# Stacks of q and k made for two heads at once and placed by transfers, in a one-core encoder layer

## The chip, the cores and the metric

One core of one Trainium2 chip runs the whole layer in one launch. The metric is the device time of an execution in microseconds; of several runs the median counts. The median of three runs of the kernel before is 787.64 us (787.47 to 788.48).

## What is computed

A post-norm encoder layer on 512 tokens of 1024 channels, in float32. Two token mixers run side by side on one input projection, a learned gate merges them, and a SwiGLU channel mixer follows.

```python
qa, ka, va, qb, kb, vb = jnp.split(h @ w_in[l], SPLITS, axis=-1)
qa = rope_partial(qa, pos); ka = rope_partial(ka, pos)      # 16 query heads, 4 kv heads of 64
qb = rope_partial(qb, pos); kb = rope_partial(kb, pos)      # 3 groups of 4 heads of 64
o_a = windowed_gqa_sink(qa, ka, va, a_sink[l])              # |i-j| <= 128, with a sink logit
o_b = dilated_mixture(qb, kb, vb)                           # (window, dilation) 128/1, 512/4, 2048/16
g_a, g_b = jnp.split(jax.nn.sigmoid(h @ w_gate[l] + b_gate[l]), 2, axis=-1)
y = (g_a * (o_a @ w_br_a[l]) + g_b * (o_b @ w_br_b[l])) @ w_out[l]
h = layer_norm(DN_ALPHA * h + y, ln1_g[l], ln1_b[l])
f = (jax.nn.silu(h @ w_ff_gate[l]) * (h @ w_ff_up[l])) @ w_ff_down[l]
h = layer_norm(DN_ALPHA * h + f, ln2_g[l], ln2_b[l])
```

## The kernel before

Every float32 product is made of reduced-precision parts. An operand x is split into hi (x rounded to the matmul's type, a copy on ScalarE or VectorE) and lo (x - hi, a subtraction on VectorE), and a product is three matmuls: hi x hi, hi x lo, lo x hi (`feat_k`, lines 441 to 456). A unit of weights is 128 output channels of one matrix: two half units of 128x512, each loaded by SP into a staging slot (6 of class "ws") and split into two weight slots (12 of class "whl"). A half unit feeds four steps of three matmuls.

The program's order is not written by hand. `Program.run` (lines 166 to 259) takes all operations with their costs and lists them as they would become ready: each engine takes, of the operations that are ready and whose buffers fit, the one with the smallest priority number. Priority numbers follow the dense products; evacuations stand 100 ahead (`EV`), weight loads and splits 130 ahead (`LOOK`). A transfer by SP is taken to hold the queue for 0.06 us and to be done after the terms of lines 232 to 236:

```python
if e == SP:
    end = now + 0.06
    dma[0] = max(dma[0], now) + 0.45
    dma[1] = max(dma[1], dma[0] + 0.65) + cost
    o.done = dma[1] + 0.9
```

The engines then run their lists in order, and semaphores keep the dependences. `ORDER` (line 75) names the order of the work: q units and k units of mixer A (q1 to q7, k1) and of mixer B (Q and K, pair and group), values (VA, V0, V12), gates (G, g) and the attention units A0 to A3 and B0 to B3.

Slots: 85 slots of 128x512 floats. 10 hold the mixers' results (`oaT`, eight, and `obT`), 16 belong to the attention, 6 and 12 to the weights, and the other 41 are general ("gen"). `fits` (line 147) lets an operation that is not the next in line take a general slot only when `spare` (14) stay free. When the last attention unit is done `free_all` raises the limit to 63 (line 916).

The change touches these parts.

- `q_post` (line 489): `rotate` makes the rotary form R of a unit's two heads, four VectorE operations (lines 471 to 477). A head's stack t holds hi in one half of the partitions and lo in the other. For each head one copy (line 498, shown under the copy helper's lines 321 and 323) and one subtraction (line 501), each on 64 partitions, put them there.
- `k_post` (line 508): for each head two copies of hi into the two halves of t, one subtraction (line 519) and one copy of lo into the other half of kl.
- `scores` (line 528) multiplies a q stack with t and with kl, at lines 535 and 536.
- `split_of` (line 923; copy 925, subtraction 926) splits a result for the merging products. Line 940 does so for mixer A's eight results `oaT`. Their products (lines 944 to 948) are shown at lines 451 to 453 with the operands `sl,sl`.
- A gate that has to wait is stored to HBM (line 853, from SP) and loaded again (line 935).

Of the kernel before, what the change touches and what calls it, by code (L numbers as in the profile page):

```python
# [10 lines left out]
F32R = mybir.dt.float32r  # L11
BF16 = mybir.dt.bfloat16
AF = mybir.ActivationFunctionType
ALU = mybir.AluOpType

P = 128
S = 512
# [4 lines left out]
NR = 4  # L22
# [23 lines left out]
PE, ACT, DVE, POOL, SP = "PE", "ACT", "DVE", "POOL", "SP"  # L46
# [7 lines left out]

N_HALF = 3
N_LAST1, N_LAST = 5, 4
BANKS = dict(dense=3, s=2, tb=2, o=1, d=8)
UNITS = 2
SPIN = 4
# [5 lines left out]
N_WS, N_WHL, N_ATT = 6, 12, 16  # L65
# [3 lines left out]
N_CHUNK, N_PAIR, N_WF, N_WS2, N_WHL1, N_WHL2 = 3, 3, 9, 10, 54, 20  # L69
# [23 lines left out]


class Op:
    __slots__ = ("alts", "fn", "prio", "left", "ready", "succ", "bufs", "new", "done", "eng", "strict", "moves", "hold")


class Program:
# [12 lines left out]
    def buf_of(tok):  # L112
        return tok[0] if isinstance(tok, tuple) else tok

    def op(self, alts, fn, reads=(), writes=(), prio=0.0, after=(), abs_prio=None, moves=0.0):
        o = Op()
        o.alts, o.fn = alts, fn
        o.prio = (self.T + prio if abs_prio is None else abs_prio, len(self.ops))
        o.ready, o.done, o.eng = 0.0, None, None
        deps = set(a for a in after if a is not None)  # L120
        for t in reads:
            deps.update(self.writer.get(t, ()))
        for t in writes:
            deps.update(self.writer.get(t, ()))
            deps.update(self.readers.get(t, ()))
        deps.discard(o)
        for t in reads:
            self.readers.setdefault(t, []).append(o)
        for t in writes:
            self.writer[t] = [o]  # L130
            self.readers[t] = []
        o.bufs, o.new = [], []
        o.strict, o.moves = self.strict, moves
        o.hold = self.hold and prio <= -150
        for t in list(reads) + list(writes):
            b = self.buf_of(t)
            if b not in o.bufs:
                o.bufs.append(b)
                b.users += 1
        o.succ = []  # L140
        o.left = len(deps)
        for d in deps:
            d.succ.append(o)
        self.ops.append(o)
        return o

    def fits(self, o):
        need = {}
        for b in o.bufs:
            if b.tile is None:  # L150
                for key in b.keys:
                    if key in self.limits:
                        need[key] = need.get(key, 0) + 1
        if "gen" in need and self.limits["gen"] - self.used["gen"] - need["gen"] < self.spare:
            while self.line and self.line[0].done is not None:
                self.line.popleft()
            if self.line and self.line[0] is not o:
                return False
        if "whl" in need and o.strict:
            while self.weights and self.weights[0].done is not None:  # L160
                self.weights.popleft()
            if self.weights and self.weights[0] is not o:
                return False
        return all(self.used[k] + n <= self.limits[k] for k, n in need.items())
# [106 lines left out]
def dve(n, fast=False, extra=0.0):  # L271
    return 0.069 + (0.00052 if fast else 0.00104) * n + extra
# [7 lines left out]
def hybrid_layer(ctx: ExitStack, tc: tile.TileContext, wpack, xT, xtok, sink, bgate,  # L280
                 ln1g, ln1b, ln2g, ln2b, ropec, ropes, maska, maskb, identd, out):
    nc = tc.nc
# [5 lines left out]
    N_SLOT = 85  # L288
    pr = Program({"slot": N_SLOT, "bank": 8, **BANKS,
                  "ws": N_WS, "whl": N_WHL, "att": N_ATT, "gen": N_SLOT - 10 - N_ATT - N_WS - N_WHL,  # L290
                  "unit": UNITS, "st": 4, "x4": 4, "wf": N_WF})
    op = pr.op
# [7 lines left out]
    def slot(dt=F32, cls=None):  # L300
        cls = cls or "gen"
        return Buf("slot", cls, lambda: slab.tile([P, S], dt, tag="slab", bufs=N_SLOT, name=name("sl")))
# [16 lines left out]
    def copy(eng, dst, src):  # L319
        if eng == ACT:  # L320
            nc.scalar.activation(dst, src, AF.Copy)  # L321
        else:
            nc.vector.tensor_copy(dst, src)

    def f32(ap):
        return ap.bitcast(F32)
# [11 lines left out]
    def cp_alts(n, ps=False, cut=0.0):  # L338
        return [(ACT, act(n, ps) + cut), (DVE, dve(n, not ps) + cut)]

    CUT = 0.12
# [73 lines left out]
    for j in range(KD):  # L415
        st, ap = slot(F32, "xs"), FIRST["x"][j]

        for c0, c1 in ((0, S // 2), (S // 2, S)) if j == 0 else ((0, S),):
            w, sk = c1 - c0, (st, c0)
            th, tl = [(b, j, c0) if j == 0 else (b, j) for b in (xh4[j // 4], xl4[j // 4])]  # L420
            eng, dma = (ACT, nc.scalar) if j == 0 and c0 == 0 else (SP, nc.sync)
# [3 lines left out]
               reads=[sk], writes=[th], abs_prio=ap)  # L425
            op([(DVE, dve(w))], lambda e, j=j, st=st, c0=c0, c1=c1: nc.vector.tensor_tensor(  # L426
                xl[j]()[:, c0:c1], st.t[:, c0:c1], f32(xh[j]()[:, c0:c1]), op=ALU.subtract), reads=[sk, th],
               writes=[tl], abs_prio=ap)
# [8 lines left out]
       reads=[nsink], writes=[nsink], abs_prio=-119)  # L437
# [26 lines left out]
    EV, NORM = -100.0, -150.0  # L464
# [4 lines left out]
    def rotate(ps):  # L469
        R, Sh = slot(), slot()  # L470
        op([(DVE, dve(S))], lambda e: nc.vector.tensor_tensor(R.t, ps.t, cosT.t, op=ALU.mult),
           reads=[ps, cosT], writes=[R], prio=EV)
        op([(DVE, dve(S, extra=0.1))], lambda e: nc.vector.stream_shuffle(Sh.t, ps.t, SHUF), reads=[ps], writes=[Sh],
           prio=EV)
        op([(DVE, dve(S))], lambda e: nc.vector.tensor_tensor(Sh.t, Sh.t, sinT.t, op=ALU.mult),
           reads=[Sh, sinT], writes=[Sh], prio=EV)
        op([(DVE, dve(S))], lambda e: nc.vector.tensor_tensor(R.t, R.t, Sh.t, op=ALU.add),
           reads=[R, Sh], writes=[R], prio=EV)
        return R

    def view(ap, nt, src):

        if nt == 0:
            return ap
        if src:
            return ap.rearrange("p (r t i) -> p t r i", r=4, t=nt)
        return ap.rearrange("p (t r i) -> p t r i", r=4, t=nt)

    def q_post(ps, nt, kv_half):

        R = rotate(ps)
        out_ = []
        for hh in range(2):
            a = 64 * hh
            hr = 64 * kv_half[hh]
            lr = 64 - hr
            t = slot(F32R)
            op(cp_alts(S, cut=CUT), lambda e, t=t, a=a, hr=hr: copy(
                e, view(t.t[hr:hr + 64], nt, False), view(R.t[a:a + 64], nt, True)),
               reads=[R], writes=[(t, "h"), (t, "room")], prio=EV)  # L500
            op([(DVE, dve(S, extra=CUT))], lambda e, t=t, a=a, hr=hr, lr=lr: nc.vector.tensor_tensor(
                view(t.t[lr:lr + 64], nt, False), view(R.t[a:a + 64], nt, True),
                view(f32(t.t[hr:hr + 64]), nt, False), op=ALU.subtract),
               reads=[R, (t, "h")], writes=[(t, "l")], prio=EV)
            out_.append((t, hr))
        return out_

    def k_post(ps, nt):

        R = rotate(ps)  # L510
        out_ = []
        for hh in range(2):
            a, c = 64 * hh, 64 - 64 * hh
            t, kl = slot(F32R), slot(F32R)
            for d, key in ((a, "h"), (c, "d")):
                op(cp_alts(S, cut=CUT), lambda e, t=t, a=a, d=d: copy(
                    e, view(t.t[d:d + 64], nt, False), view(R.t[a:a + 64], nt, True)),
                   reads=[R], writes=[(t, key), (kl, "room" + key)], prio=EV)
            op([(DVE, dve(S, extra=CUT))], lambda e, t=t, kl=kl, a=a: nc.vector.tensor_tensor(
                view(kl.t[a:a + 64], nt, False), view(R.t[a:a + 64], nt, True),  # L520
                view(f32(t.t[a:a + 64]), nt, False), op=ALU.subtract),
               reads=[R, (t, "h")], writes=[(kl, "h")], prio=EV)
            op(cp_alts(S), lambda e, kl=kl, a=a, c=c: copy(e, kl.t[c:c + 64], f32(kl.t[a:a + 64])),
               reads=[(kl, "h")], writes=[(kl, "d")], prio=EV)
            out_.append((t, kl))
        return out_

# [116 lines left out]
    oaT = [slot(F32, "res") for _ in range(8)]  # L644
# [221 lines left out]
    psk, psq, psv = bank("dense"), bank("dense"), bank("dense")  # L866
    for k in range(KD):
        for w, ps in (("k", psk), ("q", psq), ("v", psv)):
            for c in (0, S // 2) if (w, k) == ("k", 0) else (None,):
                if c is None:  # L870
                    feat_k(ps, [first[w, 0], first[w, 1]], k, XM, xtok_of, split=w == "k")
                else:
                    feat_k(ps, [first[w, 0], first[w, 1]], k, XM, lambda k, c=c: [(xh4[0], 0, c), (xl4[0], 0, c)],
                           n0=c, n1=c + S // 2, begins=c == 0, split=True)
    ka = k_post(psk, 4)
    qa = q_post(psq, 4, (0, 0))
    load(mB, maskb, prio=0)
    env = {"gate": 0, "qs": {}, "ks": {}}

# [40 lines left out]
    op([(POOL, 0.0)], free_all, after=lasts)  # L920


    def split_of(src, toks, prio=0.0):
        h, l = slot(F32R), slot(F32R)
        op(cp_alts(S), lambda e: copy(e, h.t, src.t), reads=toks, writes=[h, (l, "room")], prio=prio)
        op([(DVE, dve(S))], lambda e: nc.vector.tensor_tensor(l.t, src.t, f32(h.t), op=ALU.subtract),
           reads=[*toks, h], writes=[l], prio=prio)
        return h, l
# [4 lines left out]
    for f, d in away.items():  # L933
        gz[f] = slot()
        op([(SP, 0.73)], lambda e, d=d, t=gz[f]: nc.sync.dma_start(t.t, d.t), reads=[d], writes=[gz[f]],
           after=exps, prio=-20)
    for f in range(16):
        op([(ACT, act(S))], lambda e, f=f: nc.scalar.activation(gz[f].t, gz[f].t, AF.Sigmoid),
           reads=[gz[f]], writes=[gz[f]], after=exps)
    sa = [split_of(t, [(t, b) for b in range(NR)], -20) for t in oaT]  # L940
    MA = moving(sa)
    sm = []
    mark = None
# [498 lines left out]
    for f in range(H, NFF):  # L1442
# [7 lines left out]
       after=[silu])  # L1450
# [110 lines left out]
```

## Time and profile before

| | before |
|---|---|
| median of 3 runs | 787.64 us (787.47 to 788.48) |
| the profiled execution | 787.02 us |
| its span, first to last instruction | 785.2 us |
| TensorE busy | 774.9 us, 99% |
| weight loads busy | 683.3 us, 87% |
| VectorE busy | 676.6 us, 86% |
| ScalarE busy | 466.6 us, 59% |
| granted TensorE clock | 0.997 |

The profile is of one execution. PE is TensorE's matmuls, PEld its weight loads, DVE VectorE, ACT ScalarE, POOL GpSimd, SP the queue that issues most transfers. Matmuls overlap, so a busy PE says that matmuls were under way, not at which pace they followed each other. Stretches are counted from the span's start. About 14 to 345 us hold the projections and the attention, 345 to 460 the merge and the first normalisation, 460 to 776 the channel mixer, and the rest the last normalisation.

### The profile page before, as it was taken

Reading aid. Unit: us, or ns where it says so; the run is one execution under the profiler, and the core shown is the slowest. Engines: PE = TensorE matmul, PEld = TensorE weight load, DVE = VectorE, ACT = ScalarE, POOL = GpSimd, SP = SyncE. Lnnn points to the kernel's source line nnn. Section 1 sums busy time; section 2 is a strip of 40 time slices with the busy share of each in tenths; the row PEclk is TensorE's granted clock in tenths of the full one; section 3 lists DMA queues with packets and bytes.
Section 4 is the critical chain, followed back from the end, with each engine's and each line's share of the span. In section 5 each row is a group of like instructions: output and inputs, shape, how many; then the busy total and the mean of one; then the engine's idle time right before and its main releaser. Section 6 shows DMA issues by size and latency. Waiting matters only on the chain.

```text
span 785.2 us, 13312 instructions
## 1 busy us (share of the span) xinstructions
PE 774.9 (99%) x4541; PEld 683.3 (87%) x4541; DVE 676.6 (86%) x1425; ACT 466.6 (59%) x1025; POOL 103.4 (13%) x272
## 2 busy tenths in 40 slices
PE   9999999999999999999999999999999999999995
PEld 6888888888888888888888899999999999999984
DVE  5899998899798599759797899798998989898977
ACT  5656777767658544778333565656566555565710
POOL 0000100000003300420020011111212201212100
PEclk9999999999999999999999999999999999999998
DMA  8633122242122212338675378665977967967402
GB/s 270 223 94 113 67 68 68 93 123 80 41 92 82 87 51 81 121 112 291 209 161 141 76 217 191 161 161 143 227 235 182 222 162 194 239 172 180 104 27 80
DMA packets 63011, 110.72 MB, mean 141 GB/s; under 512 B 7136, under 2 KB 11104, under 8 KB 62944
## 3 DMA queue, kind: packets, MB, share of 16 engines
q1 hardware_dynamic: 53008, 91.92, 35.8%
q0 software_dynamic: 9792, 17.83, 14.2%
q8 instruction: 35, 0.57, 0.3%
q14 instruction: 32, 0.26, 0.1%
q10 hardware_dynamic: 144, 0.13, 0.0%
HBM read 105.40 MB, written 4.46 MB: 140 GB/s over the span
## 4 chain that ended last, share of the span: by engine, by line
PE 93%; DVE 3%; ACT 1%; SPq 1%; DMA 1%; issue 1%; DVEq 0%; ACTq 0%
PE ps L451 12%; PE ps L452 12%; PE ps L453 12%; PE ps L1207 9%; PE ps L1209 9%; PE ps L1208 9%; PE ps L1418 4%; PE ps L1417 4%; PE ps L1419 4%; PE ps L635 3%; PE ps L996 2%; PE ps L995 2%; PE ps L994 2%; PE ps L536 2%; PE ps L535 2%; PE ps L681 1%
## 5 line engine op out<-in xcount | busy, mean ns | idle before, releaser
L321 ACT ACTIVATE sl<-sl 128x512 fp32r<-128x512 f32 (+3 forms) x420 | 235.5, 591 | 73.2 <-DVE sl L1097 23.1
L1097 DVE TENSOR_TENSOR sl<-sl,sl 128x512 fp32r<-128x512 f32 (+3 forms) x294 | 166.4, 608 | 6.9 <-ACT sl L321 5.9
L321 ACT ACTIVATE sl<-ps 128x256 f32<-128x256 f32 (+4 forms) x184 | 82.0, 457 | 115.3 <-PE ps L1209 71.7
L451 PE MATMUL ps<-x,sl 128*128 128x512 f32 (+1 forms) x337 | 134.4, 399 | 0.1
L452 PE MATMUL ps<-x,sl 128*128 128x512 f32 (+1 forms) x337 | 131.8, 391 | 0.2 <-DVE x L426 0.2
L453 PE MATMUL ps<-x,sl 128*128 128x512 f32 (+1 forms) x337 | 131.5, 390 | 0.0
L1207 PE MATMUL ps<-sl,sl 128*128 128x256 f32 x352 | 99.8, 283 | 0.2 <-ACT sl L321 0.2
L1209 PE MATMUL ps<-sl,sl 128*128 128x256 f32 x352 | 99.6, 283 | 0.0
L1208 PE MATMUL ps<-sl,sl 128*128 128x256 f32 x352 | 99.6, 283 | 0.0
L347 DVE TENSOR_TENSOR sl<-sl,sl 128x512 fp32r<-128x512 f32 x130 | 87.4, 685 | 12.1 <-ACT sl L321 9.2
L453 PEld LDWEIGHTS ps<-x,sl 128*128 128x128 f32 x337 | 63.3, 188 | 14.0 <-DVE sl L370 0.2
L1207 PE MATMUL ps<-x,sl 128*128 128x256 f32 x264 | 74.7, 283 | 0.0
L1209 PE MATMUL ps<-x,sl 128*128 128x256 f32 x264 | 74.7, 283 | 0.0
L1208 PE MATMUL ps<-x,sl 128*128 128x256 f32 x264 | 74.7, 283 | 0.0
L451 PEld LDWEIGHTS ps<-x,sl 128*128 128x128 f32 x337 | 63.5, 188 | 12.1 <-ACT sl L321 0.7
L452 PEld LDWEIGHTS ps<-x,sl 128*128 128x128 f32 x337 | 63.6, 189 | 12.0 <-DVE x L426 1.3
L335 POOL DMA_DIRECT2D sl<-wpack x44 | 39.1, 907 | 257.0 <-DVE sl L1097 130.8
L1207 PEld LDWEIGHTS ps<-sl,sl 128*128 128x128 f32 x352 | 67.5, 192 | 1.1 <-ACT sl L321 0.6
L1208 PEld LDWEIGHTS ps<-sl,sl 128*128 128x128 f32 x352 | 67.5, 192 | 0.4
L1209 PEld LDWEIGHTS ps<-sl,sl 128*128 128x128 f32 x352 | 67.5, 192 | 0.0
L1208 PEld LDWEIGHTS ps<-x,sl 128*128 128x128 f32 x264 | 50.6, 192 | 0.6
L1207 PEld LDWEIGHTS ps<-x,sl 128*128 128x128 f32 x264 | 50.6, 192 | 0.6
(135 smaller groups left out, 1631.4 us busy)
## 6 DMA issues: line engine op xcount, KB each, us to landing
sl<-wpack SPq DMA_DIRECT2D x243, 256.0 KB, 3.6
wf<-wpack SPq DMA_DIRECT2D x51, 256.0 KB, 4.7
sl<-wpack POOLq DMA_DIRECT2D x44, 256.0 KB, 5.1
wf<-wpack POOLq DMA_DIRECT2D x24, 256.0 KB, 5.4
gz<-sl SPq DMA_DIRECT2D x9, 256.0 KB, 2.2
sl<-gz SPq DMA_DIRECT2D x9, 256.0 KB, 5.1
sl<-xtok SPq DMA_DIRECT2D x8, 256.0 KB, 6.3
sl<-xT SPq DMA_DIRECT2D x7, 256.0 KB, 5.4
```

What stands on the lines that cost most here:

```text
L321: nc.scalar.activation(dst, src, AF.Copy)
L335: op([(POOL, 1.0)], lambda e: nc.gpsimd.dma_start(b.t, src2, accum_op=ALU.add), reads=[b], writes=[b], prio=prio, moves=1.65)
L347: op([(DVE, dve(S))], lambda e: nc.vector.tensor_tensor(l.t, src.t, f32(h.t), op=ALU.subtract), reads=[src, h], writes=[l], prio=prio, abs ...
L451: mm(o, a, x0, start=(k == 0 and begins), stop=False, skip_group_check=split)
L452: mm(o, a, x1, start=False, stop=False, skip_group_check=split)
L453: mm(o, b, x0, start=False, stop=(k == nk - 1), skip_group_check=split)
L1097: op([(DVE, dve(w))], lambda e: nc.vector.tensor_tensor(dst(), x(), y(), op=o), reads=reads, writes=writes, prio=prio)
L1207: mm(o, wh, bh[k](), start=(first and k == 0), stop=False, skip_group_check=True)
L1208: mm(o, wh, bl[k](), start=False, stop=False, skip_group_check=True)
L1209: mm(o, wl, bh[k](), start=False, stop=(k == 3), skip_group_check=True)
L1417: mm(ps.t, x0, w[0].t, start=(first and m == 0), stop=False, skip_group_check=True)
L1418: mm(ps.t, x0, w[1].t, start=False, stop=False, skip_group_check=True)
```

## The change

`q_post` and `k_post` now make hi and lo of both heads at once, on 128 partitions, in two slots x and y, and SP moves rows of 64 partitions of them into the stacks: four transfers for a q unit, eight for a k unit. The first k and q units keep the old functions, renamed `k_near` and `q_near`. For mixer A's results an early split must leave four more general slots free, and each finished split raises the limit of general slots by one.

```diff
+SPARE_OUT = 4
...
-        if "gen" in need and self.limits["gen"] - self.used["gen"] - need["gen"] < self.spare:
+        if "gen" in need and self.limits["gen"] - self.used["gen"] - need["gen"] < self.spare + o.extra:
...
-    def q_post(ps, nt, kv_half):
+    def q_near(ps, nt, kv_half):
...
-    def k_post(ps, nt):
+    def k_near(ps, nt):
...
+    def both_parts(ps, nt):
+
+        R = rotate(ps)
+        x, y = slot(F32R), slot(F32R)
+        op(cp_alts(S, cut=CUT), lambda e: copy(e, view(x.t, nt, False), view(R.t, nt, True)),
+           reads=[R], writes=[x, (y, "room")], prio=EV)
+        op([(DVE, dve(S, extra=CUT))], lambda e: nc.vector.tensor_tensor(
+            view(y.t, nt, False), view(R.t, nt, True), view(f32(x.t), nt, False), op=ALU.subtract),
+           reads=[R, x], writes=[y], prio=EV)
+        return x, y
+
+    def move(dst, d, src, c, key, rooms=()):
+
+        op([(SP, 0.4)], lambda e: nc.sync.dma_start(f32(dst.t[d:d + 64]), f32(src.t[c:c + 64])), reads=[src],
+           writes=[(dst, key), *rooms], prio=EV)
+
+    def q_post(ps, nt, kv_half):
+
+        x, y = both_parts(ps, nt)
+        out_ = []
+        for a in (0, 64):
+            t = slot(F32R)
+            move(t, a, x, a, "h", [(t, "room")])
+            move(t, 64 - a, y, a, "l")
+            out_.append((t, a))
+        return out_
+
+    def k_post(ps, nt):
+
+        x, y = both_parts(ps, nt)
+        out_ = []
+        for a in (0, 64):
+            t, kl = slot(F32R), slot(F32R)
+            for b, src in ((t, x), (kl, y)):
+                for d, key in ((a, "h"), (64 - a, "d")):
+                    move(b, d, src, a, key, [(kl, "room" + key)] if b is t else [])
             out_.append((t, kl))
         return out_
...
-    ka = k_post(psk, 4)
-    qa = q_post(psq, 4, (0, 0))
+    ka = k_near(psk, 4)
+    qa = q_near(psq, 4, (0, 0))
...
-    sa = [split_of(t, [(t, b) for b in range(NR)], -20) for t in oaT]
+
+    def give_room(e):
+        pr.limits.update(gen=min(pr.limits["gen"] + 1, N_SLOT - N_WS2 - N_WHL))
+
+    sa = []
+    for t in oaT:
+        sa.append(split_of(t, [(t, b) for b in range(NR)], -20, SPARE_OUT))
+        op([(POOL, 0.0)], give_room, after=pr.writer[sa[-1][1]])
```

## Rows read from the trace of the kernel before

**Rows 1.** The page, busy time of each engine.
```profile
PE 774.9 (99%) x4541; PEld 683.3 (87%) x4541; DVE 676.6 (86%) x1425; ACT 466.6 (59%) x1025; POOL 103.4 (13%) x272
```

**Rows 2.** Busy times by stretch: stretch, its length, engines in us, granted clock, DMA share, GB/s.
```profile
0.00:14.00 14.00, 12.45 (x44) 7.46 (x45) 7.42 (x20) 7.89 (x16) 0.20 (x4) 1.00 0.71 232
...
34.00:240.00 206.00, 206.00 (x1031) 174.04 (x1030) 187.63 (x454) 142.09 (x322) 14.61 (x58) 1.00 0.27 86
240.00:345.00 105.00, 105.00 (x572) 90.27 (x571) 79.73 (x211) 63.81 (x159) 28.29 (x134) 1.00 0.29 93
345.00:460.00 115.00, 114.92 (x605) 98.26 (x604) 98.01 (x171) 61.25 (x122) 8.88 (x10) 1.00 0.57 163
460.00:776.00 316.00, 315.79 (x2207) 296.42 (x2207) 281.12 (x532) 177.47 (x385) 50.43 (x58) 1.00 0.68 174
776.00:785.30 9.30, 0.76 (x4) 0.30 (x2) 5.73 (x11) 0.29 (x1) 0.00 (x0) 0.72 0.30 113
```

**Rows 3.** Waits of TensorE, the longest: us in total, times, longest us.
```profile
PE ps L397 <- DVE eps L438: 1.2, 1, 1.2
```

**Rows 4.** Order of time, 40 to 46 us, TensorE: start us, us, what.
```profile
41.23 0.39 PE L453 MATMUL ps<-x,sl 128*128 128x512 f32 x1
41.45 0.40 PE L451 MATMUL ps<-x,sl 128*128 128x512 f32 x1
41.46 0.19 PEld L452 LDWEIGHTS ps<-x,sl 128*128 128x128 f32 x1
```

**Rows 5.** Groups by line and form, 34 to 345 us: busy us, mean ns.
```profile
L321 ACT ACTIVATE sl<-sl 128x512 fp32r<-128x512 f32 x83 | 50.5, 621 | 0.2
L321 ACT ACTIVATE sl<-sl 64x512 fp32r<-64x512 f32 x49 | 30.8, 629 | 12.7 <-DVE sl L477 10.3 <-DVE sl L519 1.6
L323 DVE CAST sl<-sl 64x512 fp32r<-64x512 f32 x19 | 8.0, 422 | 0.5
L501 DVE TENSOR_TENSOR sl<-sl,sl 64x512 fp32r<-64x512 f32 x27 | 18.5, 687 | 0.9
L519 DVE TENSOR_TENSOR sl<-sl,sl 64x512 fp32r<-64x512 f32 x14 | 9.6, 686 | 0.4
L926 DVE TENSOR_TENSOR sl<-sl,sl 128x512 fp32r<-128x512 f32 x5 | 3.4, 678 | 0.0
```

**Rows 6.** Transfers issued from 34 to 345 us: count, KB each, us to landing.
```profile
sl<-wpack SPq DMA_DIRECT2D x87, 256.0 KB, 3.1
gz<-sl SPq DMA_DIRECT2D x9, 256.0 KB, 2.2
sl<-gz SPq DMA_DIRECT2D x9, 256.0 KB, 5.1
```

**Rows 7.** Order of time, 54 to 75 us, SP's queue.
```profile
54.68 1.83 SPq L329 DMA_DIRECT2D sl<-wpack  x4
...
68.88 0.33 SPq L853 DMA_DIRECT2D gz<-sl  x1
```

**Rows 8.** Waits of SP's queue, 15 to 345 us: total us, times, longest.
```profile
SPq L853 <- ACT sl L849: 111.6, 9, 19.6
...
SPq L329 <- DMA sl<-wpack: 1.0, 3, 0.3
```

**Rows 9.** Order of time: ends of rotations and first scores behind them.
```profile
234.83 0.69 DVE L477 TENSOR_TENSOR sl<-sl,sl 128x512 f32<-128x512 f32 x1
...
241.44 0.25 PE L535 MATMUL ps<-sl,sl 128*128 128x192 f32 x1
...
313.89 0.69 DVE L477 TENSOR_TENSOR sl<-sl,sl 128x512 f32<-128x512 f32 x1
...
318.00 0.25 PE L535 MATMUL ps<-sl,sl 128*128 128x192 f32 x1
```

**Rows 10.** Order of time, 340 to 362 us: a split of a result and a product.
```profile
346.60 0.69 DVE L926 TENSOR_TENSOR sl<-sl,sl 128x512 fp32r<-128x512 f32 x1
...
356.87 0.39 PE L451 MATMUL ps<-sl,sl 128*128 128x512 f32 x1
```

More of the change, by code (lines that the diff above doesn't have):

```diff
@@ L95 @@
 class Op:
-    __slots__ = ("alts", "fn", "prio", "left", "ready", "succ", "bufs", "new", "done", "eng", "strict", "moves", "hold")
+    __slots__ = ("alts", "fn", "prio", "left", "ready", "succ", "bufs", "new", "done", "eng", "strict", "moves", "hold", "extra")
 class Program:
@@ L113, in buf_of, with op @@
         return tok[0] if isinstance(tok, tuple) else tok
-    def op(self, alts, fn, reads=(), writes=(), prio=0.0, after=(), abs_prio=None, moves=0.0):
+    def op(self, alts, fn, reads=(), writes=(), prio=0.0, after=(), abs_prio=None, moves=0.0, extra=0):
         o = Op()
@@ L132, in op @@
         o.bufs, o.new = [], []
-        o.strict, o.moves = self.strict, moves
+        o.strict, o.moves, o.extra = self.strict, moves, extra
         o.hold = self.hold and prio <= -150
@@ L524, in k_post @@
                reads=[(kl, "h")], writes=[(kl, "d")], prio=EV)
+            out_.append((t, kl))
+        return out_
[19 more added lines that the diff above has]
+            out_.append((t, a))
+        return out_
+    def k_post(ps, nt):
[6 more added lines that the diff above has]
+                    move(b, d, src, a, key, [(kl, "room" + key)] if b is t else [])
             out_.append((t, kl))
@@ L920, in hybrid_layer, with split_of @@
     op([(POOL, 0.0)], free_all, after=lasts)
-    def split_of(src, toks, prio=0.0):
+    def split_of(src, toks, prio=0.0, extra=0):
         h, l = slot(F32R), slot(F32R)
-        op(cp_alts(S), lambda e: copy(e, h.t, src.t), reads=toks, writes=[h, (l, "room")], prio=prio)
+        op(cp_alts(S), lambda e: copy(e, h.t, src.t), reads=toks, writes=[h, (l, "room")], prio=prio, extra=extra)
         op([(DVE, dve(S))], lambda e: nc.vector.tensor_tensor(l.t, src.t, f32(h.t), op=ALU.subtract),
```

## The prediction

> **What bounds the kernel now.** I read the page's list of engines first: TensorE is busy for 774.9 of 785.2 us, VectorE for 86% [rows 1]. Then the busy times by stage: from 34 to 776 us TensorE is busy 206.00 of 206.00, 105.00 of 105.00, 114.92 of 115.00 and 315.79 of 316.00 us, at a granted clock of 1.00, which is the upper level of 2.4 GHz [rows 2]. So 0.08 + 0.21 = 0.29 us are idle. Outside lie the start (1.55 of its 14 us idle) and the last normalisation (9.3 us after the last products), and no edit touches either. Third, what TensorE waited for: its longest wait, 1.2 us, is the warm-up's [rows 3]. Busy matmuls overlap, so a short wait could hide in these rows. Therefore the order of time: 128x512 matmuls start 0.22 us apart, each 0.39 to 0.40 long [rows 4], so a wait longer than about 0.17 us opens a gap that the rows above would show. They show almost none: TensorE's stream of products is the bound in every stage.
>
> By its busy VectorE looks near a bound too: 187.63 of 206.00 us in the first attention stretch [rows 2]. But nothing on TensorE waits for it there, so its time is cover, not path.
>
> The Trainium skill, "Perfetto Trace Analysis", section "Identifying the Most-Contended Engine", says that matmul busy is no measure of how near TensorE is to its limit and asks for the busy share of weight loads. By that rule the 87% of this trace leave some 102 us of room, which relief elsewhere might open. The trace disagrees: a load takes 0.19 us and the next 512-column matmul starts 0.22 us after the last [rows 4]; 0.19/0.22 is 86%, and 174.04 of 206.00 us is 84% [rows 2], so the share is what a stream without gaps gives.
>
> **The change part by part.** *Arithmetic on VectorE and ScalarE.* The new posts serve 13 q units (q1 to q7, six Q) and 7 k units (k1, six K); the first k and q keep the old ones. In the stretch from 34 us on stand 49 + 19 = 68 copies of 64 partitions and 27 + 14 = 41 subtractions, one of which still belongs to the first q [rows 5]. That agrees with the code: 13 x 2 + 7 x 6 copies, 13 x 2 + 7 x 2 subtractions. Removed: 30.8 + 8.0 + 26 x 0.687 + 9.6 = 66.3 us. An instruction on 64 partitions costs as much as one on 128: 629 against 621 ns for a copy on ScalarE, 687 against 678 ns for a subtraction [rows 5]. Added: 20 copies x 0.62 + 20 subtractions x 0.68 = 26.0 us. Net 40.3 us less, about 22 of it on VectorE if ScalarE takes all copies, 13 if VectorE does. What hides these 40 us today is TensorE's stream, so they are worth **0 us**; the most they can give is the idle time of the stage they lie in, and this is 0.00 [rows 2].
>
> *The 108 transfers.* 13 x 4 + 7 x 8 = 108 moves of 64 x 2 KB (128 KB) join SP's queue among its 87 + 18 transfers of that stretch [rows 6]. Issue: four loads in a row take 1.83 us, a lone store 0.33 [rows 7], so 108 take 36 to 50 us of SP's 311. Bytes: 108 x 0.131 = 14.2 MB in 311 us are 46 GB/s beside 86 to 93 GB/s that keep the DMA engines 27 to 29% busy [rows 2], so about 14 points more. Neither is near full. A move waits in SP's queue for its copy or subtraction, and the weight loads queue up behind it; the products are what waits for those. The cover is what is fetched ahead: 12 weight slots are six half units, each 12 matmuls of 0.22 us, so 16 us, and six more loads are staged. The trace has a harder case: SP stands at the gates' stores for 111.6 us in nine waits, up to 19.6 us each [rows 8], with loads behind, and TensorE does not notice. **0 us.**
>
> *Latency of a stack.* Before, from the end of the rotation to the first score that needs the last part: K02's ends at 234.83 + 0.69 = 235.52, B0's first score is at 241.44, 5.9 us; K12's ends at 314.58 and B2, which needs its first head alone, begins at 318.00, 3.4 us [rows 9]. After, copy and subtraction take 0.62 + 0.69 = 1.31 us, the low parts are issued 0.46 us apart (two for one head, four for both), and then they land. No row shows a transfer inside SBUF. The nearest: 2.2 us for the stores of a slot, 3.1 for the weight loads, 5.1 for nine loads in a burst [rows 6]. With 2.2 to 5.1: K02 1.31 + 3 x 0.46 + landing, 4.9 to 7.8 us; K12's first head 1.31 + 0.46 + landing, 4.0 to 6.9. Against today that is from 1.0 us early to 3.5 us late. (Elsewhere a unit of mixer A or another dense product lies between.) But the order is listed anew with the moves in it: lines 232 to 236 hold a score back for 0.45 + 0.65 + 0.4 + 0.9 = 2.4 us per move, and dense products go ahead of it. Only what the chip takes beyond 2.4 us can stop TensorE. I take 2.2, the row that leaves SBUF and reads no weights, so **0 us**; the upper end is 5.1 - 2.4 = 2.7 us at each of the two places, 5.4 us.
>
> The Trainium skill, "SBUF — State Buffer", section "Door 1: The DMA port swizzle", speaks against the change: partitions 0 to 63 reach eight of the 16 ports and 64 to 127 the other eight, so a transfer of 64 partitions has half the bandwidth. No transfer of this trace has 64 partitions, so no row shows it. By it a move would cost what a whole slot costs, and the fourth move of a group would come later than by the sum above.
>
> *Slots of mixer A's split results.* The general slots are 85 - 10 - 16 - 6 - 12 = 41. Before, a split was listed out of turn while the others held 25 - 2k (k splits done); now it is 21 - k: stricter for the first four, the same for the fifth, looser after. In the trace five of these splits come before 345 us [rows 5], a sixth at 346.60, and mixer A's dense products run again at 356.87 [rows 10]. With the looser limit the last of the eight come earlier. The price they can earn is the 0.08 us idle there [rows 2]: **-0.1 us.**
>
> Sum: 0 + 0 + 0 - 0.1. The profiled execution took 787.02 us (span 785.2, 1.8 around it), so 786.9; the median of the runs is 0.62 us over it, so **787.5**.
>
> **The rivals.** *A, slower: late moves.* The low parts land later than the order assumes, and a score at the head of TensorE's queue stops everything behind it. Places: K02 before unit B0, K12 before B2. For it: an issue on SP already waits now and then for an earlier transfer to land [rows 8], groups of eight moves would do so more often, and burst landings are 5.1 us [rows 6]. Against it: the calm rows, 2.2 and 3.1. It decides from the point where landing takes over 2.4 us. One late place is 2.7 us: **790.2**; both, 792.9. Chance 0.13. The page's halved bandwidth would work by this same mechanism.
>
> *B, faster: VectorE was the bound.* If the busy 91% of the first stretch really held TensorE up, 13 us or more would come off: **774**. For it only VectorE's share; against it 206.00 of 206.00. By the page on weight loads this should happen, and by the rows it can't. Chance 0.04 for all over 0.2% faster.
>
> *C, slower: the splits come later, not earlier.* The first four have the stricter limit. If the room is never there out of turn, three more copies and subtractions (0.42 + 0.69 each) fall where products have run out, at 345 to 357 us: +3.3 us, **790.8**. Against it: the limit grows with each split. Chance 0.05.
>
> **How the numbers follow.** 0.2% (1.6 us) is about what a measurement of this kernel can tell from no change. Within it: the forecast, 0.78. Slower: A and C, 0.18. Faster: 0.04. The range begins at 786.6 (the profiled 787.02 less all 0.29 us of idle, less the 0.17 by which the lowest run shown lies under the median) and reaches to 790.2, one late place; beyond it lie both places late.
>
> **What would show it.** Right: copies and subtractions of these lines on 128 partitions, 20 each; VectorE 13 to 22 us less busy between 34 and 345 us; 108 moves from SP with a median landing under 2.4 us; TensorE still 206.00 of 206.00; all splits of mixer A before 345 us. Wrong: a gap on TensorE ahead of scores that a move ended (A), one at 340 to 357 us ended by a split (C), or fewer microseconds between the start and the last product without any gap having been there (B).

## The result: slower by 0.19%, and the profile after

The kernel after takes 789.44 us (median of 12 runs, 788.69 to 790.37) beside 787.88 for the kernel before (12 runs, 787.28 to 788.70). The ratio is 1.0019, 95% interval 1.0011 to 1.0026. The forecast was no change at 787.5. The loss lies inside the range and just under the 0.2% that was called no change, but its interval excludes zero. In a second series, described with the experiments, the ratio was 1.0011 (1.0002 to 1.0020). So the change costs 1.6 us in one series and 0.8 in the other; each series has its own runs of the kernel before, whose medians lie between 787.79 and 788.25.

The profiled execution took 789.72 us, its span is 787.9. First the page's list of engines, which answers to [rows 1].

```profile
PE 775.3 (98%) x4541; PEld 683.0 (87%) x4541; DVE 660.1 (84%) x1402; ACT 438.3 (56%) x980; POOL 103.6 (13%) x272
```

VectorE is 16.5 us and ScalarE 28.3 us less busy, TensorE as busy as before. The busy times by stretch, as in [rows 2], say where TensorE stood.

```profile
34.00:240.00 206.00, 204.08 (x1023) 171.88 (x1022) 178.36 (x445) 128.27 (x305) 14.15 (x60) 1.00 0.42 122
240.00:345.00 105.00, 105.00 (x567) 90.08 (x566) 73.47 (x199) 52.02 (x135) 28.88 (x132) 1.00 0.55 156
345.00:460.00 115.00, 114.76 (x594) 97.62 (x594) 94.94 (x168) 58.38 (x117) 8.82 (x10) 1.00 0.56 161
```

The first stretch has 1.92 us of idle where there was none. The others differ from before by 0.16 us at most (the last, from 460 us, is 315.79 of 316.00 as before). TensorE's waits name what ended it:

```profile
PE ps L608 <- DVE sl L324: 1.0, 1, 1.0
PE ps L575 <- DVE sl L476: 0.6, 1, 0.6
```

Beside the warm-up's, as in [rows 3], two places are new. L608, the values' transposes at 35 us, lies ahead of the first instruction in which the two programs differ (SP's queue at 37 us, the computing engines from 44 us on); whether it belongs to the change is a question for the runs. L575 is `scores` (L535 before): mixer A's first attention unit A0, the first user of q1's stacks. The order of time of TensorE there:

```profile
50.67 0.39 PE L454 MATMUL ps<-x,sl 128*128 128x512 f32 x1
51.66 0.35 PE L575 MATMUL ps<-sl,sl 128*128 128x256 f32 x1 [0.60 <-DVE sl L476]
51.85 0.28 PE L576 MATMUL ps<-sl,sl 128*128 128x256 f32 x1
52.44 0.35 PE L575 MATMUL ps<-sl,sl 128*128 128x256 f32 x1 [0.31 <-DMA sl<-sl]
52.63 0.28 PE L576 MATMUL ps<-sl,sl 128*128 128x256 f32 x1
```

Starts are to be read, not busy times: a 512-column product is followed after 0.23 us and a 256-column one after 0.12 when nothing is late. The distances 0.99, 0.19, 0.59 and 0.19 us exceed that by 0.76, 0.07, 0.47 and 0.07, so this stop costs 1.37 us. The profile puts the first part down to VectorE, but L476 had ended at 51.17, half a microsecond ahead of the score; the transfers of q1 show what was late. SP's queue in that stretch:

```profile
46.03 1.16 SPq L542 DMA_DIRECT2D sl<-sl  x2
47.29 0.54 SPq L330 DMA_DIRECT2D sl<-wpack  x1
47.92 1.10 SPq L542 DMA_DIRECT2D sl<-sl  x2
```

The four moves of q1 are the two pairs at L542: high parts, then one 256 KB weight load, then the low parts. The transfers issued between 47.8 and 49 us, count, KB each and median us to landing, are that second pair:

```profile
sl<-sl SPq DMA_DIRECT2D x2, 128.0 KB, 3.8
```

They were issued at 47.92 and 48.44. Taken singly they land 3.65 and 3.87 us later, at 51.56 and 52.30, and the two scores start 0.10 and 0.14 us after that. Over all transfers from 34 to 345 us the median looks harmless:

```profile
sl<-sl SPq DMA_DIRECT2D x108, 128.0 KB, 2.4
```

It hides a wide spread: 46 of the 108 land more than 3 us after their issue. The four issued from 318 us on are the slowest group:

```profile
sl<-sl SPq DMA_DIRECT2D x4, 128.0 KB, 4.7
```

TensorE stops for none of these but q1's. A late landing alone is not a stop; at the other places there are products enough to cover it.

### The profile page after: what moved, and what is told of

It is laid out like the page before. It is cut to its first block, busy times and chain, and to the rows that moved or that the text cites. A ratio compares the mean times of both kernels' runs of the same rounds, so it can differ in the third digit from the quotient of the medians.

```text
span 787.9 us, 13485 instructions
## 1 busy us (share of the span) xinstructions
PE 775.3 (98%) x4541; PEld 683.0 (87%) x4541; DVE 660.1 (84%) x1402; ACT 438.3 (56%) x980; POOL 103.6 (13%) x272
## 4 chain that ended last, share of the span: by engine, by line
PE 89%; DVE 4%; DMA 3%; ACT 2%; issue 1%; SPq 1%; DVEq 0%; ACTq 0%
PE ps L452 10%; PE ps L454 10%; PE ps L453 10%; PE ps L1254 9%; PE ps L1256 9%; PE ps L1255 9%; PE ps L1465 4%; PE ps L1464 4%; PE ps L1466 4%; PE ps L675 3%; PE ps L1043 2%; PE ps L1041 2%; PE ps L1042 2%; PE ps L576 2%; PE ps L575 2%; ACT sl L322 1%
## 5 line engine op out<-in xcount | busy, mean ns | idle before, releaser
L322 ACT ACTIVATE sl<-sl 128x512 fp32r<-128x512 f32 (+3 forms) x385 | 212.7, 587 | 101.3 <-DVE sl L478 38.3
L322 ACT ACTIVATE sl<-ps 128x256 f32<-128x256 f32 (+5 forms) x182 | 80.0, 454 | 118.1 <-PE ps L1256 71.9
L454 PEld LDWEIGHTS ps<-x,sl 128*128 128x128 f32 x337 | 63.3, 188 | 13.9 <-DVE sl L371 0.2
L453 PEld LDWEIGHTS ps<-x,sl 128*128 128x128 f32 x337 | 63.5, 188 | 11.7 <-DVE x L427 1.3
L452 PEld LDWEIGHTS ps<-x,sl 128*128 128x128 f32 x337 | 63.4, 188 | 11.8 <-ACT x L322 1.0
L707 ACT ACTIVATE sl<-sl,st 128x257 f32<-128x257 f32 (+1 forms) x64 | 35.6, 558 | 28.1 <-DVE st L703 25.0
L1255 PEld LDWEIGHTS ps<-x,sl 128*128 128x128 f32 x264 | 50.6, 192 | 0.6
```

Source lines behind the costliest of these rows:

```text
L452: mm(o, a, x0, start=(k == 0 and begins), stop=False, skip_group_check=split)
L453: mm(o, a, x1, start=False, stop=False, skip_group_check=split)
L454: mm(o, b, x0, start=False, stop=(k == nk - 1), skip_group_check=split)
L707: exps.append(op([(ACT, act(n + 1, extra=2))], lambda e, p=p, h=h: nc.scalar.activation(p.t[:, :n + 1], p.t[:, :n + 1], AF.Exp, bias=st.t[ ...
L1255: mm(o, wh, bl[k](), start=False, stop=False, skip_group_check=True)
```

## The experiments

The theory before the first of them: the whole loss is the stop ahead of A0's first scores, made by q1's low parts, which queue behind a weight load. The rivals: the start is what differs (the values' transposes), the new order costs elsewhere, or the slots do.

**The change again.** The kernel after, unchanged, to see what of its profile repeats.

> The changed kernel again, as the mark for the others. Theory (the low parts of q1 land late ahead of unit A0, and that is all the loss): 1.4 to 1.7 us over before, and the profile shows the gap of about 1.4 us at the first scores that need q1 (50 to 53 us). The wait of 1.2 us ahead of the transposes of the values (35 us) lies before the first instruction in which the two programs differ, so by the theory it comes and goes with the start of an execution and need not be there again. Rival (that wait belongs to the change): it is there again, 1.0 to 1.2 us, in each profile with the change.

789.08 us (788.35 to 789.81, 11 runs) beside 788.25 before (33 runs); ratio 1.0011 (1.0002 to 1.0020). Its waits:

```profile
PE ps L608 <- DVE sl L324: 0.6, 1, 0.6
PE ps L575 <- DVE sl L476: 0.3, 1, 0.3
```

By starts the stop ahead of A0 is 0.86 us (0.45 + 0.07 + 0.27 + 0.07). The low parts land after 3.3 us here, 0.4 less than in the first profile (3.34 beside 3.76), and the stop is 0.5 us shorter. Both waits repeat, smaller than in the first profile, and the stop is smaller than the 1.4 us that was expected. Why the same program's moves landed sooner in this execution no run shows.

**q1 the old way.**

```diff
-            qa.extend(dense_q(U_QA + i, 4, (kv, kv)))
+            if i == 1:
+                ps = bank("dense")
+                feat_x(ps, unit(U_QA + i))
+                qa.extend(q_near(ps, 4, (kv, kv)))
+            else:
+                qa.extend(dense_q(U_QA + i, 4, (kv, kv)))
```

> The change, but q1 keeps the old form (parts made in place, no transfers); 104 of the 108 moves stay. Theory: the gap at A0's scores is gone and the time falls by 1.3 to 1.5 us, to within 0.3 us of before. Rival (108 moves crowd the queue and the weights come late all over the attention): the time falls by under 0.2 us, since 96% of the moves are still there.

788.22 us (787.77 to 789.13), ratio 1.0003 (0.9994 to 1.0012): no loss is left that the runs can tell, with 4 of the 108 moves gone. TensorE from 44 to 60 us has no idle:

```profile
44.00:60.00 16.00, 16.00 (x79) 13.54 (x78) 14.98 (x39) 12.29 (x30) 0.89 (x4) 1.00 0.30 77
```

**The load behind.** All 108 moves stay; SP may not list a weight load in the stretch of the listing in which q1's moves stand, so it comes after them.

```diff
                     o = best
                     cost = dict(o.alts)[e]
+                    if e == SP and cost == 0.73 and 43.5 < now < 44.8:
+                        continue
```

> The change, with one line more in the listing: the weight load that stands in SP's queue between q1's high and low parts is listed behind the low parts. Nothing else of the moves is changed. Theory (the load in front is what makes the low parts late: 3.7 to 3.9 us to landing behind it, 2.3 without): the low parts land in about 2.3 us, about 2 us earlier; the gap at A0's scores shrinks from 1.4 to under 0.3 us, the time falls by 1.1 to 1.5 us. Rival (a transfer of 64 partitions is slow by itself, whatever stands in front): landing still over 3 us, gap over 1 us, time unchanged within 0.3 us.

788.35 us (787.32 to 788.95), ratio 1.0002 (0.9993 to 1.0011). The order of time of SP's queue and of TensorE (line numbers are two higher here):

```profile
45.38 2.44 SPq L544 DMA_DIRECT2D sl<-sl  x4
47.92 1.50 SPq L332 DMA_DIRECT2D sl<-wpack  x3
...
50.02 0.39 PE L456 MATMUL ps<-x,sl 128*128 128x512 f32 x1
50.24 0.28 PE L577 MATMUL ps<-sl,sl 128*128 128x256 f32 x1
...
50.48 0.28 PE L577 MATMUL ps<-sl,sl 128*128 128x256 f32 x1
```

The transfers issued from 44 to 50 us, with their landing last:

```profile
sl<-sl SPq DMA_DIRECT2D x4, 128.0 KB, 2.3
```

With the same moves and the same work, one load put behind them takes the landing from 3.8 to 2.3 us and the scores follow at pace. The low parts also leave SP sooner, 1.26 us after the first high part instead of 1.89. This is the run that tells the load from the moves.

**A later place in the list.** The moves of q1 are entered dearer, so the listing holds the scores back and puts dense products ahead.

```diff
-        op([(SP, 0.4)], lambda e: nc.sync.dma_start(...
+        op([(SP, cost)], lambda e: nc.sync.dma_start(...
...
-            qa.extend(dense_q(U_QA + i, 4, (kv, kv)))
+            qa.extend(dense_q(U_QA + i, 4, (kv, kv), 0.9 if i == 1 else 0.4))
```

> The change, with q1's four moves entered in the list at a cost of 0.9 instead of 0.4 us each, so that A0's scores that need them are listed 1.4 to 2.4 us later, behind two dense products. The transfers themselves are as late as before. Theory (the loss is the list's, which holds the score back for too short a time): no gap at A0's scores although landing is as slow as in the change, and the time falls by 1.2 to 1.5 us to within 0.3 us of before. Rival (there is no other work that can fill the time, so the wait only moves): a gap of over 1 us elsewhere between 45 and 60 us, and the time unchanged.

A miss in the time: 789.33 us (788.67 to 789.85), ratio 1.0014 (1.0005 to 1.0023). The stop ahead of A0 is gone, as expected, though the low parts still land after 3.5 us. But the new listing stops TensorE in another place, where the merged results are late for the output projection. The profile names VectorE's product L1008; in the order of time the last stop ends with the split's copy on ScalarE (405.91 to 406.54, the matmul starts at 406.53), which follows VectorE's addition:

```profile
PE ps L1041 <- DVE sl L1008: 0.8, 1, 0.8
```

By starts that is 0.23 + 1.01 = 1.24 us at 404 us. Every entry in the list relists what follows, 350 us later too, so a time after such an edit is not the price of the edit alone.

**The slots alone.** All stacks the old way; only `give_room` and `SPARE_OUT` are left.

```diff
-        return q_post(ps, nt, kv_half)
+        return q_near(ps, nt, kv_half)
...
-        return k_post(ps, nt)
+        return k_near(ps, nt)
```

> All stacks are made the old way, by four narrow operations and no transfer; only the giving back of slots behind mixer A's splits is left of the change. Theory (the whole loss is the stop of TensorE ahead of mixer A's first scores, which the transfers of the second q make): no stop there, 787.9 to 788.5 us beside 788.2 before, the same within 0.2%. Rival (the new order of the list behind the slots costs the time): slower by 0.8 us or more, with stops of TensorE after 340 us that the profile of before doesn't have. Second rival (the slots alone gain): 0.3 us or more faster.

788.48 us (788.00 to 789.58) beside 787.97 (15 runs): ratio 1.0008 (0.9999 to 1.0017). No gain, and no stop ahead of A0. In part the rival's sign is there: this listing too stops at the output projection (0.6 us by the waits, 0.86 by starts), as neither before nor the change does.

```profile
PE ps L1041 <- DVE sl L1008: 0.6, 1, 0.6
```

**A first dose, spoilt.** Each low-part transfer of q1 issued twice.

```diff
+        def go(e):
+            for _ in range(times):
+                nc.sync.dma_start(f32(dst.t[d:d + 64]), f32(src.t[c:c + 64]))
...
-            move(t, 64 - a, y, a, "l")
+            move(t, 64 - a, y, a, "l", times=2 if twice else 1)
```

> The change, with the two low-part transfers of the second q of mixer A issued twice each, at the same place of the list: one dose more of what the theory blames. Theory: two transfers more lie behind the same weight load, each takes SyncE 0.5 to 0.6 us and the landings come 0.45 to 0.9 us apart, so the stop of TensorE ahead of the scores grows from 0.9 to 1.4 us to 1.8 to 2.6 us, and the time from 789.1 or 789.4 to 790 to 790.6 us. Rival (the stop is there but is made up for later, and the loss has another cause): the stop grows, the time stays at 789.1 to 789.5 us. Rival (other waits set the scores' start): the stop stays at 0.9 to 1.4 us.

795.19 us (794.98 to 796.60, 4 runs), ratio 1.0094 (1.0080 to 1.0107), far above what either theory gave. The edit was not the dose it was meant to be: the second copy writes the rows of the first, so SP waits for the first to land. SP issues the four at 48.77, 52.04, 52.56 and 54.93. TensorE's waits (`scores` is L578 here):

```profile
PE ps L578 <- issue: 2.5, 1, 2.5
PE ps L578 <- DMA sl<-sl: 2.4, 1, 2.4
```

The busy times of the same kernel by stretch (the granted clock stands third from the end):

```profile
54.00:56.00 2.00, 0.47 (x2) 0.30 (x2) 1.12 (x4) 0.60 (x2) 0.00 (x0) 0.81 0.19 42
56.00:58.00 2.00, 0.73 (x3) 0.76 (x4) 0.57 (x1) 0.63 (x2) 0.00 (x0) 0.50 0.83 243
...
60.00:62.00 2.00, 2.00 (x6) 1.52 (x6) 1.31 (x4) 1.23 (x3) 0.00 (x0) 0.50 0.03 8
```

There are two stops of 2.6 us by starts, with two products between them, and after the first the granted clock falls to 0.50, the level of 1.2 GHz, until 62 us; 512-column products then follow each other 0.43 us apart instead of 0.23. From 40 to 80 us the starts lose 7.8 us over pace, against 1.7 in the change: 6.1 us more, and the time rose by 5.8 over the change's 789.44. It speaks against one rival: nothing of such a stop seems to be made up for later.

**The kernel before, profiled again.**

> The kernel of before, profiled a second time. At 35 us, ahead of the first instruction in which the two programs differ, the changed kernel's profiles show TensorE waiting up to 1.2 us at the values' transposes. Theory (this wait comes and goes with an execution's start): 0 to 1.2 us of it here too. Rival (it belongs to the change): none, as in the first profile of before. In both cases no stop ahead of mixer A's first scores and 787.2 to 788.8 us.

788.25 us. The wait at the values' transposes is here as well, longer than in any profile of the change:

```profile
PE ps L568 <- DVE sl L323: 1.3, 1, 1.3
```

It comes and goes from execution to execution of the same program: 0 and 1.51 us by starts in the two profiles of the kernel before. That rival falls, and with it half of the 1.92 us of idle in the profile after.

**Transfers alone.** A kernel of transfers that computes nothing of the layer: groups of eight, 64 rows within their half ("low"), 64 rows across ("cross"), the same 128 KB as 128 rows of half the columns ("half"), whole tiles ("full"), 256 KB loads, and a load with two moves after it ("mixed").

> A kernel of transfers alone, each group ended before the next begins; it computes nothing of the layer. Theory A (a 64-row transfer between two tiles in SBUF is bound by a fixed time): alone 2.0 to 2.4 us from issue to landing, eight in a row 0.45 to 0.6 us apart, that is at SyncE's pace, the same whether they stay in their half of the partitions or cross to the other, and not slower than the same 128 KB as 128 rows of half the columns. Theory B (64 partitions reach half of the ports): eight of 64 rows take twice the time, landing to landing, of eight with 128 rows and half the columns. Of the mixed group both say: behind one 256 KB weight load the two 64-row transfers land 3.0 to 3.9 us after their issue if they queue behind the load, 2.0 to 2.5 us if they don't.

Transfers: count, KB each, us to landing.

```profile
full<-src SPq DMA_DIRECT2D x8, 256.0 KB, 2.6
low<-src SPq DMA_DIRECT2D x8, 128.0 KB, 2.3
cross<-src SPq DMA_DIRECT2D x8, 128.0 KB, 2.3
half<-src SPq DMA_DIRECT2D x8, 128.0 KB, 2.1
```

The groups by line, of two groups the eight additions behind the transfers: busy us, mean ns, idle before them, and its releaser.

```profile
L29 DVE TENSOR_TENSOR src<-src,low 128x512 f32<-128x512 f32 x8 | 5.5, 692 | 7.1 <-DMA low<-src 6.8
L29 DVE TENSOR_TENSOR src<-src,half 128x512 f32<-128x512 f32 x8 | 5.5, 692 | 6.8 <-DMA half<-src 6.6
```

Eight transfers on 64 partitions take 6.8 us, eight of the same bytes on 128 take 6.6: not twice. Either kind follows at SP's pace, 0.64 us from issue to issue, so these groups show that SP and not a port sets their pace; a halved rate below that pace they could not show. The "mixed" group is a miss of the design: its moves waited for an addition and were issued 1.45 us after the load, when that was nearly done, and landed after 2.2.

**Behind a load, back to back.** Groups that are issued without a wait between them, each twice: two moves ("alone"); a load and two ("one"); the order at q1 ("q"); the order of the run with the load behind ("swap"); two loads and two ("two").

```diff
+        run("alone", ["hiA", "hiB"])
+        run("one", ["loadA", "loA", "loB"])
+        run("q", ["hiA", "hiB", "loadA", "loA", "loB"])
+        run("swap", ["hiA", "hiB", "loA", "loB", "loadA"])
+        run("two", ["loadA", "loadB", "loA", "loB"])
```

> Transfers alone again, now issued back to back with no wait between them; it computes nothing of the layer. Five groups, each twice: two 64-row transfers; a 256 KB load and then two; two, a load, two more (the order at the second q); two, two more and then the load (the order of the run with the load behind); two loads and then two. Theory (each DMA engine works off its packets in the order of issue, so a transfer waits for what lies ahead of it): alone 2.2 to 2.4 us from issue to landing; behind one load 3.0 to 3.9; in the second q's order 3.3 to 3.9; with the load last 2.2 to 2.5; behind two loads 3.6 to 4.6. Rival (the long landings come from other traffic in the kernel, or from the source of the load there): 2.2 to 2.5 us in all groups.

```profile
alonehiA<-src SPq DMA_DIRECT2D x2, 128.0 KB, 2.2
...
oneloA<-src SPq DMA_DIRECT2D x2, 128.0 KB, 3.3
...
qloA<-src SPq DMA_DIRECT2D x2, 128.0 KB, 3.5
...
swaploA<-src SPq DMA_DIRECT2D x2, 128.0 KB, 2.3
...
twoloA<-src SPq DMA_DIRECT2D x2, 128.0 KB, 4.1
```

All five groups are where the theory put them. A load directly ahead costs a move 1.1 us of landing, a second one 0.8 more, with none of the layer's work beside it. The Trainium skill, "DMA: Bandwidth & Descriptors", section "Queues, rings and completion order", says that each DMA engine takes the descriptors of a queue in their order; these rows agree. (In the kernel the low parts took 3.8 and 3.3 us, on either side of the "q" group.)

**The dose again.** Two transfers of 64 rows into a tile that nothing reads, right ahead of q1's low parts.

```diff
+    scratch = slab.tile([P, S], F32, tag="scratch", bufs=1, name="scratch")
...
+            for r in ((0, 64) if more else ()):
+                nc.sync.dma_start(scratch[r:r + 64], f32(src.t[r:r + 64]))
+            nc.sync.dma_start(f32(dst.t[d:d + 64]), f32(src.t[c:c + 64]))
```

> The dose again, free of the wait that spoilt the first one (there each second copy wrote the rows of the first and so waited for its landing): the change, with two transfers more of 64 rows into a tile that nothing reads, issued right ahead of the two low-part transfers of the second q. Theory (issue at SyncE plus landing set the stop): the low parts are issued 1.1 to 1.25 us later, the stop ahead of the scores grows from 0.7 to 1.2 us (two profiles of the change, sum of both waits over pace) to 1.8 to 2.6 us, the granted clock stays whole, and the time is 1.0 to 1.6 us over the change's 789.1 to 789.4: 790.1 to 791.0 us. Rival (the stop is made up for further on): the stop grows, the time stays within 0.4 us of the change. If the granted clock falls behind the longer stop, as it did behind the 5 us of the first dose, the time is 791.5 us or more.

790.11 us (789.02 to 791.02, 9 runs) beside 787.79 (13 runs): ratio 1.0028 (1.0018 to 1.0038), at the lower edge of what the theory gave, 790.1 to 791.0. The order of time of SP's queue and of TensorE (the moves are L547 here, `scores` L581):

```profile
46.17 0.54 SPq L330 DMA_DIRECT2D sl<-wpack  x1
46.80 1.10 SPq L546 DMA_DIRECT2D scratch<-sl  x2
47.95 1.24 SPq L547 DMA_DIRECT2D sl<-sl  x2
...
49.55 0.39 PE L454 MATMUL ps<-x,sl 128*128 128x512 f32 x1
51.34 0.36 PE L581 MATMUL ps<-sl,sl 128*128 128x256 f32 x1 [1.40 <-issue]
...
51.89 0.35 PE L581 MATMUL ps<-sl,sl 128*128 128x256 f32 x1
```

The transfers issued from 47.9 to 49 us, which are the low parts:

```profile
sl<-sl SPq DMA_DIRECT2D x2, 128.0 KB, 3.2
```

The two extra transfers put the low parts 1.15 us later in SP's queue (46.80 to 47.95), these land 3.2 us after that, and the stop is 1.56 + 0.07 + 0.24 + 0.07 = 1.95 us, at a granted clock of 1.00.

**The account.** For each profile at full clock: the span; the time that TensorE lost in the first 20 us (distances of starts less the pace, summed over all products there); the stops at the values, ahead of A0 and at the output projection, by starts; and what is left of the span.

| kernel | span | first 20 us | values | A0 | 404 us | left |
|---|---|---|---|---|---|---|
| before | 785.2 | 3.59 | 0 | 0 | 0 | 781.6 |
| before, again | 786.5 | 3.32 | 1.51 | 0 | 0 | 781.7 |
| after | 787.9 | 3.61 | 1.18 | 1.37 | 0 | 781.7 |
| after, again | 787.5 | 4.12 | 0.81 | 0.86 | 0 | 781.7 |
| q1 the old way | 786.6 | 4.26 | 0.28 | 0 | 0 | 782.1 |
| load behind | 786.0 | 3.88 | 0.28 | 0 | 0 | 781.8 |
| later in the list | 788.0 | 3.80 | 1.21 | 0 | 1.24 | 781.8 |
| slots alone | 786.6 | 3.16 | 0.93 | 0 | 0.86 | 781.7 |
| dose | 787.2 | 3.70 | 0 | 1.95 | 0 | 781.6 |

Nothing is missing from the account: all nine spans agree within 0.5 us once the start and these stops are taken off. The first two columns of losses vary from execution to execution of either kernel. The two others appear in some listings only, and their size varies with the execution (1.37 and 0.86 us of one program).

## Why the prediction was wrong

**TensorE as the bound: right.** It still stands at 105.00 of 105.00 us, and the time moves by its stops and by nothing else. So the rejected rule on weight loads' busy share stays rejected: relief elsewhere opened no time.

**Arithmetic: right.** 34 to 345 us has 20 subtractions on 128 partitions and 16 more such copies on ScalarE than [rows 5].

```profile
L322 ACT ACTIVATE sl<-sl 128x512 fp32r<-128x512 f32 x99 | 59.6, 622 | 36.1 <-DVE sl L478 36.1
L535 DVE TENSOR_TENSOR sl<-sl,sl 128x512 fp32r<-128x512 f32 x20 | 13.7, 686 | 0.7 <-ACT sl L322 0.5
```

VectorE is 15.5 us less busy there (9.27 + 6.26, forecast 13 to 22) and ScalarE 25.6, together 41.1 against the 40.3 of the sum. They are worth nothing, as forecast: the run with the load behind keeps all of this relief and is level with before.

**The 108 transfers: right in the result, low in the terms.** Issue costs SP more than the loads' rate gave:

```profile
L542 SPq DMA_DIRECT2D sl<-sl x108: 461/547/1476, 46.0 to 320.2; - x108
```

At the median of 0.547 us that is 59 us, not 36 to 50. The median landing, which was to be under 2.4 us, is 2.4. The DMA share of the stretch rose from 0.28 to 0.46, 18 points instead of 14. No weight was late for it.

**Latency of a stack: this step failed.** "Only what the chip takes beyond 2.4 us can stop TensorE. I take 2.2, the row that leaves SBUF and reads no weights, so 0 us". The choice of row was right for a move alone: 2.2 to 2.3 us in the transfers by themselves. It was wrong for a move behind a weight load, and a nearer row was at hand, the weight loads' 3.1 [rows 6]. In the listing the low parts wait for the subtraction, a load is ready meanwhile and goes ahead, and they land after 3.8 and 3.3 us in the two profiles. On the chip they need not have waited, for q1's subtraction ends at 47.17, before SP issues the load at 47.29:

```profile
46.49 0.68 DVE L535 TENSOR_TENSOR sl<-sl,sl 128x512 fp32r<-128x512 f32 x1
```

The listing holds SP's queue for 0.06 us per transfer, where the chip takes 0.46 to 0.60 for nearly all; that can account for a pause on SP in the listing that the chip doesn't have, but no run tests it. The stop follows the landing: 3.8 - 1.37 and 3.3 - 0.86 are both 2.4 us, and with the dose, whose low parts are issued 1.15 us later, 3.2 + 1.15 - 1.95 is 2.4 too. So the order had left 2.4 us from issue to landing, the figure that the prediction read from lines 232 to 236, though for a move behind a load those lines add up other terms as well, so that the two figures agree stays unexplained.

The second half of the step failed too: "the upper end is 5.1 - 2.4 = 2.7 us at each of the two places". The stop is at a third place, A0's first scores behind q1, which the prediction passed over with "Elsewhere a unit of mixer A or another dense product lies between". Dense products do lie between there, up to 50.67 us, and not enough of them. At the places named nothing stopped. Behind K12 the order of time shows why: the last rotation, the four moves, the first score of B2.

```profile
313.41 0.69 DVE L478 TENSOR_TENSOR sl<-sl,sl 128x512 f32<-128x512 f32 x1
...
314.85 2.39 SPq L542 DMA_DIRECT2D sl<-sl  x4
...
320.02 0.25 PE L575 MATMUL ps<-sl,sl 128*128 128x192 f32 x1
```

The score begins 5.9 us after the rotation's end instead of 3.4 [rows 9], with other products ahead of it: the listing had done there what the prediction counted on.

**Halved bandwidth: not seen.** The Trainium skill, "SBUF — State Buffer", section "Door 1: The DMA port swizzle", gives 64 partitions half of the ports. By that a move would have cost what a whole slot costs. The transfers alone don't show that price at this size: 2.3 us for 64 rows, 2.1 for the same bytes on 128, 2.6 for a whole slot. Whether the 0.2 us between the first two are the ports', no run separates. The late landings at q1 have the load ahead as their cause: with it behind, the same 64 rows land after 2.3 us.

**Slots, -0.1: not earned.** Seven subtractions of this kind (L966) stand before 345 us instead of five [rows 5] and the next follows at 346.74, nearly as forecast, but the idle from 345 to 460 us went from 0.08 to 0.24 us. Its one wait in the list, 0.2 us, ended with ScalarE's L663 and not with a split. The run with the slots alone gained nothing either.

**The rivals.** A had the mechanism, with 0.13 for it, and the wrong place and size: one late place of 0.9 to 1.4 us instead of 2.7. B is refuted by 41 us of relief without effect. C's stop at 345 to 357 us did not occur. What no rival named is that a listing made anew can be late anywhere, as at 404 us in two of the runs; which choice of the listing decides that was not followed up.

## What to carry to other kernels

Where the bound engine runs without gaps, relief for its neighbours is worth nothing, and a change is worth only the waits it adds: look for the first consumer of each new transfer, in program order, and not just for the tightest place of the old trace. The latency of a transfer is its own plus what was issued ahead of it in its queue: where a listing lets a small move wait for data, a bulk load goes ahead of it, and holding that load back until the move is issued recovered the loss here, within the noise. In a kernel whose order a program lists, check each profile for stops far from the edit before a time is put down to the edit.

## What the runs showed of the hardware

- In the transfers alone, a 64-row, 128 KB transfer within SBUF landed 2.2 to 2.3 us after its issue, 3.3 behind one 256 KB load and 4.1 behind two. It did not matter whether the rows changed their half of the partitions.
- In the transfers alone, issue of such a move took SP 0.46 to 0.53 us for the first of a row and 0.60 for each further one; a load with no transfer just ahead of it took 0.33 to 0.39.
- Inside the layer 46 of 108 such moves landed more than 3 us after their issue, a group of four as late as 4.7.
- Behind two stops of 2.6 us with two products between them the granted clock stood at 0.50 until 62 us; behind the dose's stop of 1.95 us and the change's 1.37 it stayed at 1.00.
